# Projections of a hybrid decoder layer: one 512-column and one 256-column pass per weight block, rewritten as three 256-column passes into one set of columns

## The chip, the cores and the metric

The kernel runs on one core of one Trainium2 chip. The metric is the device time of one execution in microseconds, the median of several runs. Engines are named as the profile names them: PE is TensorE's matmuls, PEld its weight loads, DVE is VectorE, ACT ScalarE, POOL GpSimd, SP SyncE (it issues nearly all DMAs). In a matmul one operand is held in the array (the weights, loaded by a LDWEIGHTS) and the other moves through it, column by column.

## What is computed

One decoder layer on 256 tokens of width 2048, in float32. Cut to what matters here:

```python
h = rmsnorm(x, pre_mix_g)
proj = h @ w_in                       # q_a, k_a, v_a, q_b, k_b, v_b, f_b
o_a = swa_sink_attention(q_a, k_a, v_a, sinks)       # 16 heads of 64, 2 kv heads, window 128
o_b = forgetting_attention(q_b, k_b, v_b, log_f)     # 16 heads of 64
mix = concat(rmsnorm(o_a), rmsnorm(o_b)) @ w_out
x = x + rmsnorm(mix, post_mix_g)
h = rmsnorm(x, pre_ffn_g)
u = causal_dwconv(h @ w_up, conv_w, conv_b)          # w_up: 2048 x 11264, width 3
gate, val = split(u, 2)
y = (gelu(gate) * val) @ w_down                      # w_down: 5632 x 2048
return x + rmsnorm(y, post_ffn_g)
```

## The kernel before

**Numbers.** Products are made from float32r parts. A value x is split into hi (x rounded to float32r, a ScalarE copy) and lo (x - hi, a VectorE subtraction). A product is the sum of three: hi by hi, hi by lo, lo by hi.

**Layout.** The normalised activations stand transposed in hT: 16 K tiles (KT) of 128 rows, each with 512 columns, namely the high parts of the 256 tokens (0:256) and their low parts (256:512). Weights come from DRAM in units of up to 1024 floats per partition (w_load, into one of five raw buffers), are cast by ScalarE into whi and subtracted by VectorE into wlo (w_split, L120 and L123), five buffers each.

**Projections.** proj_T makes 256 output columns (two blocks m of 128) from four units of four K tiles each. The weights are held, hT moves. For every K tile and block, high() lets all 512 columns of hT pass the high weights into a bank of 512 columns: the left half collects hi by hi, the right half hi by lo. low() lets the 256 high columns pass the low weights into the right half of the same bank. So a projection uses two PSUM banks, one a block, and 32 matmuls of 512 columns (L264) and 32 of 256 (L271). In the feed-forward stage the order is LONG: high of units 0 and 1, low of all four, high of 2 and 3. In the attention stage it is high 0, 1, low 0, 1, high 2, 3, low 2, 3. The first two projections (keys and values, first queries) run through unit_T (L227, L232) interleaved with the arrival of x. The first gate projection of the feed-forward has an order of its own (first_gate, L911 and L916).

**Where the weights lie.** The high half starts at the start of its tile. The low half of a held unit starts LOW[i] * 4 floats into its tile, which is 128 floats longer than needed:

```python
LOW = (14, 4, 4, 4)
...
        at = LOW[unit[0] % period[0]] * 4
```

The counter starts anew with each projection; its period is four in the feed-forward stage and two in the attention stage.

**Evacuation.** Both halves of a bank have to be added and multiplied by the tokens' 1/rms, which is a row (rowq, rowk, rowf) because tokens are columns here. evac_sum (L417 to L419) and conv (L856 to L858) do it in three steps for each block: ScalarE copies the right half out, VectorE adds the left half to it, GpSimd multiplies by the row. Then come the split into parts (attention) or the convolution, GELU and gating (feed-forward).

**Other matmuls.** The values' projection, w_out and w_down let the weights move and hold activations (mm3 at L286, products at L1032). Some blocks of w_down go through a seven-product scheme (seven), for which GpSimd and VectorE make sums and differences beforehand; stage() prepares part of these in DRAM.

**Order.** TensorE's order is the program's (a manual schedule). tick() and later() place the attention's steps between the passes of projections. The other engines' order comes from the scheduler, pinned at some places. PSUM has four banks tagged acc and four tagged att; feed-forward projections alternate between the two.

Of the kernel before, what the change touches and what calls it, by code (L numbers as in the profile page):

```python
# [28 lines left out]
STORED = (((0, 0, 1), (0, 0, 3), (0, 0, 5), (0, 2, 1), (0, 2, 3), (0, 2, 5), (1, 0, 1)), ((1, 0, 3), (1, 2, 0), (1, 2, 1), (1, 2, 2)))  # L29
LOW = (14, 4, 4, 4)  # L30
ROOM = 112
# [3 lines left out]
def hybrid_layer(ctx: ExitStack, tc: tile.TileContext, x, pre_mix_g, w_in, b_forget, sinks,  # L35
# [42 lines left out]

    unit, period = [0], [2]

    def w_parts(n, keep=None, held=True):

        if keep and keep[0] is None:
            return keep[1]
        where, pre, nb = (keep[0], "h", keep[1]) if keep else (wp, "w", WB)
        hi = where.tile([P, UNIT], F32R, tag=pre + "hi", bufs=nb, name="whi")
        if where is not wp:
            lo = where.tile([P, UNIT], F32R, tag=pre + "lo", bufs=nb, name="wlo")
# [130 lines left out]

    def unit_T(parts, u, banks, ticks=True, halves=False):  # L220

        hi, lo = parts

        def high(a):
            kt = u * 4 + a
            for m, b in enumerate(banks):
                pe.matmul(b, hi[:, a, m * P:(m + 1) * P], hT[:, kt, 0:512], start=(kt == 0),  # L227
                          stop=(kt == KT - 1))

        def low(a):  # L230
            for m, b in enumerate(banks):
                pe.matmul(b[:, 256:512], lo[:, a, m * P:(m + 1) * P],  # L232
                          hT[:, u * 4 + a, 0:256], start=False, stop=False)
# [12 lines left out]
        if ticks:  # L246
            tick()

    def proj_T(w, c0, banks, runs=((0, 1), (0, 1), (2, 3), (2, 3))):

        parts, last = {}, ((len(runs) - 1) % 2, KT - 1)
        unit[0], period[0] = 0, 4 if len(runs) == 3 else 2

        def get(u):
            if u not in parts:
                parts[u] = w_split(w_load(w_rows(w, u * 4, 4, c0, 256), 4, 256))
            return parts[u]

        def high(u):
            hi = get(u)[0]  # L260
            for a in range(4):
                kt = u * 4 + a
                for m, b in enumerate(banks):
                    pe.matmul(b, hi[:, a, m * P:(m + 1) * P], hT[:, kt, 0:512], start=(kt == 0),  # L264
                              stop=(last == (0, kt)))

        def low(u):
            lo = get(u)[1]
            for a in range(4):
                for m, b in enumerate(banks):  # L270
                    pe.matmul(b[:, 256:512], lo[:, a, m * P:(m + 1) * P],  # L271
                              hT[:, u * 4 + a, 0:256], start=False,
                              stop=(last == (1, u * 4 + a)))
# [18 lines left out]
    with tc.tile_pool(name="mixp", bufs=1) as mp:  # L292
# [37 lines left out]
        def scratch():  # L330
            rot[0] += 1
            i = 6 + rot[0] % 10
            return scr[:, i * 256:(i + 1) * 256]

# [10 lines left out]
        warm_up(2)  # L345
        bkv = [bank("att"), bank("att")]
        bq0 = [bank(), bank()]
        for u in range(4):
# [72 lines left out]
        def q_pair(b):  # L421
            q = scratch()
            evac_sum(b, q, rowq)
            qh = ap.tile([P, 256], F32R, tag="qh", bufs=6, name="qh")
            ql = ap.tile([P, 256], F32R, tag="ql", bufs=6, name="ql")
            split(qh, ql, q)
            return qh, ql

        def k_pair(b, i):
            k = scratch()  # L430
            evac_sum(b, k, rowk)
            split(khi[i], klo[i], k)

        tiles = (1, slice(0, 256)), (0, slice(256, 384))

        def attend(j, q, ki, values, table, h0, sink, at):
# [53 lines left out]
            def pv():  # L490
# [10 lines left out]
                if sink:  # L501
                    half = ap.tile([64, 512], F32, tag="half", bufs=1, name="half")
                    act.copy(half, o[64:128, :])
                    ob = scratch()
                    for e in range(2):
# [65 lines left out]
        def kv_a():  # L571
            k32 = scratch()
            evac_sum(bkv[0], k32, rowk)
            ksw = scratch()
# [5 lines left out]
            v32 = scratch()  # L580
            evac_sum(bkv[1], v32, rowk)

# [10 lines left out]
        for g in range(4):  # L593
            if g == 0:
                b2 = bq0
            else:
                b2 = [bank(), bank()]
                proj_T(w_in, g * 256, b2)
            for m in range(2):
                swa_pair(2 * g + m, q_pair(b2[m]), stages(6 + 8 * g, m))  # L600

# [59 lines left out]
        for g in range(4):  # L661
            bq = [bank(), bank()]
            proj_T(w_in, 1280 + g * 256, bq)
            qs = [q_pair(b) for b in bq]
            bk = [bank(), bank()]
            proj_T(w_in, 2304 + g * 256, bk)
            for m in range(2):
                ki = (2 * g + m + 2) % NK
                k_pair(bk[m], ki)
                fox_pair(2 * g + m, qs[m], ki, stages(5, m))  # L670

# [112 lines left out]

        unit[0], period[0] = 0, 4

        def gate_unit(u):
# [34 lines left out]
    with tc.tile_pool(name="ffn", bufs=1) as fp:  # L822
# [21 lines left out]

        NU = 4
        ubuf = [fp.tile([P, 258], F32, tag=f"u{i}", name=f"u{i}") for i in range(NU)]
        for u in ubuf:
            pool.memset(u[:, 0:2], 0.0)
        cnt = [0]
        x_dram = tc.dram_tile([2 * P, D], F32, name="x_dram")  # L850

        def conv(b, ch, y):
            u = ubuf[cnt[0] % NU]
            cnt[0] += 1
            c = fp.tile([P, 256], F32, tag="cs", bufs=3, name="cs")
            act.copy(c, b[:, 256:512])  # L856
            dve.tensor_tensor(u[:, 2:258], b[:, 0:256], c, op=ALU.add)  # L857
            pool.tensor_tensor(u[:, 2:258], u[:, 2:258], rowf, op=ALU.mult)  # L858
            act.activation(y, u[:, 2:258], AF.Identity, bias=cw[:, 3, ch:ch + 1],  # L859
# [78 lines left out]
        for half in range(2):  # L938
            G = [fp.tile([P, 512], F32R, tag="G", bufs=FHALF, name=f"G{j}")[:, 0:512]
                 for j in range(FHALF)]  # L940
            most = max(len(at) for at in SEVENS[half])
            both = min(len(at) for at in SEVENS[half])
            sums = []

            def sums_at(u):
                w, at = 384 if u < both else 512, 768 * min(u, both) + 1024 * max(u - both, 0)
                if not u:
# [8 lines left out]
            for g in range(FHALF // 2):  # L956
                c0 = (half * (FHALF // 2) + g) * 256
                alt = (g + half) % 2
                if half == 0 and g == 0:
                    bg = first_gate()  # L960
                    order.__exit__(None, None, None)
                    bv = [bank(), bank()]
                    proj_T(w_up, DFF + c0, bv, LONG)
                else:
                    bg = [bank("att"), bank("att")] if alt else [bank(), bank()]
# [3 lines left out]
                for m in range(2):  # L969
                    y = conv(bg[m], c0 // P + m, yy[:, m, :])  # L970
                    act.activation(y, y, AF.Gelu_apprx_tanh)
                    gates.append(y)
                if half or g:
                    bv = [bank("att"), bank("att")] if alt else [bank(), bank()]
                    proj_T(w_up, DFF + c0, bv, LONG)
                ys = []
                for m in range(2):
                    y = conv(bv[m], 44 + c0 // P + m, yy[:, 2 + m, :])
                    dve.tensor_tensor(y, y, gates[m], op=ALU.mult)
                    ys.append(y)  # L980
                if g < most:
# [5 lines left out]
                    s2, s3, s4, s1 = (s[:, i * P:i * P + P] for i in range(4))  # L987
                    if g < both:
                        s1 = a21
# [54 lines left out]
            def seven(n, u, last, banks, opened):  # L1044
# [11 lines left out]
                s2, s3, s4, s1 = [  # L1056
                    [x[:, i * P:i * P + P] for x in sums[1 + u]] if i < 3 or u >= both
                    else parts_of(u * 2, 1) for i in range(4)]
# [164 lines left out]
        for n in range(4):  # L1223
            finish(0, slice(n * 512, (n + 1) * 512), r, sp)
        last = fp.tile([P, 256], F32, tag="cs", bufs=3, name="last")
        for h in range(2):
# [40 lines left out]
```

## Time and profile before

| what | value |
|---|---|
| time, median of 3 runs | 1053.36 us (1053.36 to 1053.54) |
| span of the profiled execution | 1051.2 us |
| PE busy | 1041.5 us (99%), 5896 matmuls |
| PEld busy | 907.5 us (86%), 5896 loads |
| DVE busy | 855.6 us (81%) |
| ACT busy | 647.8 us (62%) |
| POOL busy | 261.2 us (25%) |
| mean granted TensorE clock | 0.999 |
| moved by DMA | 238.82 MB |

The profiled execution's span is 2.2 us below the median time, which also has what lies around the span. Busy times are unions of an engine's instructions. A matmul's own duration runs to its modelled end, so matmuls overlap in the rows; how fast they follow each other is read from the starts, and in the view of the chain, whose pieces run from start to start. A row "x32" in the timeline merges 32 instructions of one line that follow each other.

### The profile page before, as it was taken

What the parts mean: (1) busy time and instruction counts of PE and PEld (TensorE: products, weight loads), DVE (VectorE), ACT (ScalarE), POOL (GpSimd) and SP (SyncE); (2) the same over time, 40 slices, a digit from 0 to 9 for tenths busy, and PEclk for the clock granted to TensorE, in tenths of its full rate; (3) what the DMA queues carried; (4) which work ended last, traced back from release to release, by engine and by line L of the source; (5) the groups of instructions that cost most, each with busy time, mean ns of one, the idle gap of its engine ahead of it and who ended that gap; (6) DMA issues with size and microseconds to landing.
All of it is one profiled execution on the core that took longest, in us unless ns stands there. A gap on an engine that the chain in (4) does not pass through costs nothing.

```text
span 1051.2 us, 16601 instructions
## 1 busy us (share of the span) xinstructions
PE 1041.5 (99%) x5896; PEld 907.5 (86%) x5896; DVE 855.6 (81%) x1407; ACT 647.8 (62%) x1109; POOL 261.2 (25%) x295
## 2 busy tenths in 40 slices
PE   9999999999999999999999999999999999999996
PEld 7889988888889988888888888888888888888886
DVE  5989877877467898989987988868888878799783
ACT  7777767676557655656555655646566565566561
POOL 4253235441122423232211000003433121200023
PEclk9999999999999999999999999999999999999999
DMA  8645666555874788888975876777767777768783
GB/s 293 195 122 176 180 201 187 181 163 161 299 242 147 261 276 278 264 273 267 306 232 160 269 270 226 248 236 222 228 214 249 249 222 229 231 194 271 243 301 123
DMA packets 187326, 238.82 MB, mean 227 GB/s; under 512 B 8268, under 2 KB 154988, under 8 KB 186348
## 3 DMA queue, kind: packets, MB, share of 16 engines
q1 hardware_dynamic: 186924, 237.37, 70.4%
q8 instruction: 46, 0.75, 0.3%
q10 hardware_dynamic: 320, 0.40, 0.1%
q14 instruction: 36, 0.29, 0.1%
HBM read 221.86 MB, written 15.75 MB: 226 GB/s over the span
## 4 chain that ended last, share of the span: by engine, by line
PE 98%; DVE 1%; issue 0%; ACT 0%; DVEq 0%; POOLq 0%; ACTq 0%
PE bank_acc L264 21%; PE bank_acc L1032 15%; PE bank_att L264 15%; PE bank_acc L286 13%; PE bank_acc L271 11%; PE bank_att L271 8%; PE bank_att L1032 5%; PE bank_att L286 1%; PE bank_att L452 1%; PE bank_att L487 1%; PE bank_att L496 1%; PE bank_acc L911 1%; PE bank_att L227 1%; PE bank_acc L227 1%; PE bank_att L498 0%; DVE wlo L123 0%
## 5 line engine op out<-in xcount | busy, mean ns | idle before, releaser
L123 DVE TENSOR_TENSOR wlo<-raw,whi 128x1024 fp32r<-128x1024 f32 (+3 forms) x317 | 390.7, 1244 | 76.2 <-ACT whi L120 69.0
L120 ACT CAST whi<-raw 128x1024 fp32r<-128x1024 f32 (+3 forms) x316 | 321.0, 1032 | 126.7 <-issue 49.0
L264 PE MATMUL bank_acc<-hT,whi 128*128 128x512 f32 x1024 | 245.5, 392 | 0.0
L264 PEld LDWEIGHTS bank_acc<-hT,whi 128*128 128x128 f32 x1024 | 188.2, 188 | 37.1
L858 POOL TENSOR_TENSOR u<-u,rowf 128x256 f32<-128x256 f32 x88 | 91.9, 1066 | 424.0 <-DVE u L857 421.1
L264 PE MATMUL bank_att<-hT,whi 128*128 128x512 f32 x704 | 165.7, 390 | 0.0
L264 PEld LDWEIGHTS bank_att<-hT,whi 128*128 128x128 f32 x704 | 130.6, 188 | 26.2
L1032 PE MATMUL bank_acc<-whi,G 128*128 128x512 f32 x424 | 139.8, 389 | 0.0
L271 PEld LDWEIGHTS bank_acc<-hT,wlo 128*128 128x128 f32 x1024 | 123.5, 188 | 3.2
L271 PE MATMUL bank_acc<-hT,wlo 128*128 128x256 f32 x1024 | 125.8, 278 | 0.0
L859 ACT ACTIVATE yy<-u,cw 128x256 f32<-128x256 f32 x88 | 53.0, 603 | 81.5 <-POOL u L858 81.5
L1032 PEld LDWEIGHTS bank_acc<-whi,G 128*128 128x128 f32 x424 | 79.6, 188 | 16.4
L271 PEld LDWEIGHTS bank_att<-hT,wlo 128*128 128x128 f32 x704 | 83.6, 188 | 1.9
L271 PE MATMUL bank_att<-hT,wlo 128*128 128x256 f32 x704 | 83.9, 277 | 0.0
L1032 PE MATMUL bank_acc<-wlo,G 128*128 128x512 f32 x212 | 82.5, 389 | 0.0
L286 PE MATMUL bank_acc<-whi,oT 128*128 128x512 f32 (+1 forms) x272 | 81.8, 379 | 0.0
L861 DVE SCALAR_TENSOR_TENSOR yy<-u,cw,yy 128x256 f32<-128x256 f32 x88 | 55.3, 634 | 13.9 <-ACT yy L859 13.6
L290 DVE TENSOR_TENSOR wlo<-raw,whi 128x1024 fp32r<-128x1024 f32 (+1 forms) x54 | 55.8, 1047 | 11.7 <-ACT whi L289 11.0
L289 ACT CAST whi<-raw 128x1024 fp32r<-128x1024 f32 (+1 forms) x54 | 47.8, 892 | 26.0 <-PE bank_acc L1032 16.8
L286 PEld LDWEIGHTS bank_acc<-whi,oT 128*128 128x128 f32 x272 | 50.2, 188 | 9.3
L286 PE MATMUL bank_acc<-wlo,oT 128*128 128x512 f32 (+1 forms) x136 | 51.2, 377 | 0.0
L286 PE MATMUL bank_acc<-whi,hT 128*128 128x384 f32 (+1 forms) x192 | 46.9, 323 | 0.0
(265 smaller groups left out, 1416.3 us busy)
## 6 DMA issues: line engine op xcount, KB each, us to landing
raw<-in_w_up_dram SPq DMA_DIRECT2D x176, 512.0 KB, 4.7
raw<-in_w_down_dram SPq DMA_DIRECT2D x68, 512.0 KB, 5.0
raw<-in_w_in_dram SPq DMA_DIRECT2D x51, 512.0 KB, 5.0
raw<-in_w_out_dram SPq DMA_DIRECT2D x32, 512.0 KB, 4.7
staged<-in_w_down_dram SPq DMA_DIRECT2D x44, 256.0 KB, 5.6
t_dram<-staged SPq DMA_DIRECT2D x22, 512.0 KB, 6.1
raw<-t_dram SPq DMA_DIRECT2D x14, 512.0 KB, 5.4
raw<-in_w_in_dram SPq DMA_DIRECT2D x16, 384.0 KB, 3.3
```

Of the source, the lines that this page charges most:

```text
L120: i1 = act.copy(hi[:, cs], raw[:, cs])
L123: i2 = dve.tensor_tensor(lo[:, cs], raw[:, cs], hi[:, cs].bitcast(F32), op=ALU.subtract)
L227: pe.matmul(b, hi[:, a, m * P:(m + 1) * P], hT[:, kt, 0:512], start=(kt == 0), stop=(kt == KT - 1))
L264: pe.matmul(b, hi[:, a, m * P:(m + 1) * P], hT[:, kt, 0:512], start=(kt == 0), stop=(last == (0, kt)))
L271: pe.matmul(b[:, 256:512], lo[:, a, m * P:(m + 1) * P], hT[:, u * 4 + a, 0:256], start=False, stop=(last == (1, u * 4 + a)))
L286: pe.matmul(b, a, r[:, cols], start=(first and i == 0), stop=(last and i == 2))
L289: act.copy(hi, src)
L290: dve.tensor_tensor(lo, src, hi.bitcast(F32), op=ALU.subtract)
L858: pool.tensor_tensor(u[:, 2:258], u[:, 2:258], rowf, op=ALU.mult)
L859: act.activation(y, u[:, 2:258], AF.Identity, bias=cw[:, 3, ch:ch + 1], scale=cw[:, 2, ch:ch + 1])
L861: dve.scalar_tensor_tensor(y, u[:, 1:257], cw[:, 1, ch:ch + 1], y, op0=ALU.mult, op1=ALU.add)
L1032: pe.matmul(b, x, r, start=b not in opened and not i, stop=closes and i == 2)
```

## The change

- proj_T and unit_T write into one bank: block m has columns m * 256 to m * 256 + 256. hi_rows makes two 256-column matmuls with the same high weights (hT's high columns, then its low columns) into the same columns; lo_rows makes the low one, again into these columns. All three products are thus summed in PSUM.
- High and low halves of a unit of w_parts share one tile, wboth, as long as the two tiles before. For held units the high half starts 16 floats (64 bytes) in, the low half at float 1024 + 80. LOW and its counter are gone. This holds for first_gate's weights too.
- evac and rows_of are one VectorE multiply of the 512-column bank by the row, which is broadcast over the two blocks. q_pairs and k_pairs handle two blocks at once. first_gate still has two banks and the three steps (sums_of).
- Scratch slots, the convolution's input tiles and the cs tile are cut anew; a small tile gap fills up the difference.

```diff
     def w_parts(n, keep=None, held=True):
...
-        lo = where.tile([P, UNIT + 128], F32R, tag=pre + "lo", bufs=nb, name="wlo")
-        at = 0
-        if held:
-            at = LOW[unit[0] % period[0]] * 4
-            unit[0] += 1
-        return hi[:, :n], lo[:, at:at + n]
+        both = wp.tile([P, 2 * UNIT + 128], F32R, tag="wboth", bufs=WB, name="wboth")
+        hi, lo = (16, UNIT + 80) if held else (0, UNIT)
+        return both[:, hi:hi + n], both[:, lo:lo + n]
...
+    def both(x, n):
+
+        return x.unsqueeze(1).to_broadcast([P, 2, n])
+
+    def hi_rows(b, hi, kt, last):
+
+        for m in range(2):
+            for i in range(2):
+                pe.matmul(b[:, m * 256:(m + 1) * 256], hi[:, m * P:(m + 1) * P],
+                          hT[:, kt, i * 256:(i + 1) * 256], start=(kt == m == i == 0),
+                          stop=last and m == i == 1, skip_group_check=True)
+
+    def lo_rows(b, lo, kt, last):
+
+        for m in range(2):
+            pe.matmul(b[:, m * 256:(m + 1) * 256], lo[:, m * P:(m + 1) * P], hT[:, kt, 0:256],
+                      start=False, stop=last and m == 1, skip_group_check=True)
...
         def high(u):
             hi = get(u)[0]
             for a in range(4):
-                kt = u * 4 + a
-                for m, b in enumerate(banks):
-                    pe.matmul(b, hi[:, a, m * P:(m + 1) * P], hT[:, kt, 0:512], start=(kt == 0),
-                              stop=(last == (0, kt)))
+                hi_rows(b, hi[:, a, :], u * 4 + a, last == (0, u * 4 + a))
 
         def low(u):
             lo = get(u)[1]
             for a in range(4):
-                for m, b in enumerate(banks):
-                    pe.matmul(b[:, 256:512], lo[:, a, m * P:(m + 1) * P],
-                              hT[:, u * 4 + a, 0:256], start=False,
-                              stop=(last == (1, u * 4 + a)))
+                lo_rows(b, lo[:, a, :], u * 4 + a, last == (1, u * 4 + a))
...
-        def evac_sum(b, dst, row):
-
-            c = scratch()
-            act.copy(c, b[:, 256:512])
-            dve.tensor_tensor(dst, b[:, 0:256], c, op=ALU.add)
-            pool.tensor_tensor(dst, dst, row, op=ALU.mult)
...
+        def evac(b, row):
+
+            dst = scratch()
+            dve.tensor_tensor(halved(dst), halved(b), both(row, 256), op=ALU.mult)
+            return dst
...
+        def rows_of(b):
+            u = ubuf[cnt[0] % NU]
+            cnt[0] += 1
+            dve.tensor_tensor(u[:, :, 2:258], b.rearrange("p (m c) -> p m c", m=2),
+                              both(rowf, 256), op=ALU.mult)
+            return [u[:, m, :] for m in range(2)]
...
```

More of the change, by code (lines that the diff above doesn't have):

```diff
@@ L84, in w_parts @@
             return keep[1]
[L85 to L88, printed above, removed]
+        if keep:
+            hi, lo = [keep[0].tile([P, UNIT], F32R, tag="h" + x, bufs=keep[1], name="w" + x)
+                      for x in ("hi", "lo")]
             return hi[:, :n], lo[:, :n]
-        lo = where.tile([P, UNIT + 128], F32R, tag=pre + "lo", bufs=nb, name="wlo")
-        at = 0
-        if held:
-            at = LOW[unit[0] % period[0]] * 4
-            unit[0] += 1
-        return hi[:, :n], lo[:, at:at + n]
+        both = wp.tile([P, 2 * UNIT + 128], F32R, tag="wboth", bufs=WB, name="wboth")
+        hi, lo = (16, UNIT + 80) if held else (0, UNIT)
+        return both[:, hi:hi + n], both[:, lo:lo + n]
     def w_high(unit, keep=None, held=True):
@@ L247, in unit_T, with proj_T @@
             tick()
-    def proj_T(w, c0, banks, runs=((0, 1), (0, 1), (2, 3), (2, 3))):
+    def proj_T(w, c0, b, runs=((0, 1), (0, 1), (2, 3), (2, 3))):
         parts, last = {}, ((len(runs) - 1) % 2, KT - 1)
-        unit[0], period[0] = 0, 4 if len(runs) == 3 else 2
         def get(u):
@@ L345, in hybrid_layer @@
         warm_up(2)
-        bkv = [bank("att"), bank("att")]
-        bq0 = [bank(), bank()]
+        bkv = bank("att")
+        bq0 = bank()
         for u in range(4):
@@ L503, in pv @@
                     act.copy(half, o[64:128, :])
[L504 removed]
+                    ob = scratch()[:, 0:256]
                     for e in range(2):
@@ L596, in hybrid_layer @@
             else:
-                b2 = [bank(), bank()]
+                b2 = bank()
                 proj_T(w_in, g * 256, b2)
-            for m in range(2):
-                swa_pair(2 * g + m, q_pair(b2[m]), stages(6 + 8 * g, m))
+            for m, q in enumerate(q_pairs(b2)):
+                swa_pair(2 * g + m, q, stages(6 + 8 * g, m))
         z = ap.tile([P, 2, H], F32, tag="z", name="z")
@@ L968, in hybrid_layer @@
                 yy = fp.tile([P, 4, 256], F32, tag="yy", bufs=2, name="yy")
-                for m in range(2):
-                    y = conv(bg[m], c0 // P + m, yy[:, m, :])
+                for m, u in enumerate(rows_of(bg) if half or g else sums_of(bg)):
+                    y = conv(u, c0 // P + m, yy[:, m, :])
                     act.activation(y, y, AF.Gelu_apprx_tanh)
@@ L973, in hybrid_layer @@
                 if half or g:
-                    bv = [bank("att"), bank("att")] if alt else [bank(), bank()]
+                    bv = bank("att") if alt else bank()
                     proj_T(w_up, DFF + c0, bv, LONG)
                 ys = []
-                for m in range(2):
-                    y = conv(bv[m], 44 + c0 // P + m, yy[:, 2 + m, :])
+                for m, u in enumerate(rows_of(bv)):
+                    y = conv(u, 44 + c0 // P + m, yy[:, 2 + m, :])
                     dve.tensor_tensor(y, y, gates[m], op=ALU.mult)
@@ L1224, in hybrid_layer @@
             finish(0, slice(n * 512, (n + 1) * 512), r, sp)
-        last = fp.tile([P, 256], F32, tag="cs", bufs=3, name="last")
+        last = fp.tile([P, 256], F32, tag="cs", bufs=1, name="last")
         for h in range(2):
```

92 lines of the change are left out of this document (44 added, 48 removed).

## The prediction

> **What bounds the kernel now.** I read the page's busy table first, then its clock row, the chain that ended last, and the costliest groups.
>
> ```profile
> PE 1041.5 (99%) x5896; PEld 907.5 (86%) x5896; DVE 855.6 (81%) x1407; ACT 647.8 (62%) x1109; POOL 261.2 (25%) x295
> ...
> PEclk9999999999999999999999999999999999999999
> ...
> PE 98%; DVE 1%; issue 0%; ACT 0%; DVEq 0%; POOLq 0%; ACTq 0%
> ...
> L264 PE MATMUL bank_acc<-hT,whi 128*128 128x512 f32 x1024 | 245.5, 392 | 0.0
> ...
> L264 PE MATMUL bank_att<-hT,whi 128*128 128x512 f32 x704 | 165.7, 390 | 0.0
> ...
> L271 PE MATMUL bank_acc<-hT,wlo 128*128 128x256 f32 x1024 | 125.8, 278 | 0.0
> ```
>
> TensorE is busy 99% of the span at full clock, it holds 98% of the chain, and its idle time before the projections' matmuls is 0.0. It is the bound nearly everywhere, so only a change in the spacing of its matmuls, or a new wait in it, moves the time. There are as many weight loads as matmuls (5896 each): a repeated weight is loaded again, so "held" saves no load. The mean durations (392, 278 ns) overlap each other; what counts is the distance from start to start. So next I read TensorE's timeline through one projection of the feed-forward stage, and from a second, narrower window the steady part of a low run.
>
> ```profile
> 364.19 7.45 PE L264 MATMUL bank_att<-hT,whi 128*128 128x512 f32 x32
> 371.48 3.82 PE L271 MATMUL bank_att<-hT,wlo 128*128 128x256 f32 x32
> 375.13 3.82 PE L264 MATMUL bank_att<-hT,whi 128*128 128x512 f32 x16
> 378.78 3.80 PE L264 MATMUL bank_acc<-hT,whi 128*128 128x512 f32 x16
> 382.42 3.82 PE L271 MATMUL bank_acc<-hT,wlo 128*128 128x256 f32 x32
> 386.07 0.40 PE L264 MATMUL bank_acc<-hT,whi 128*128 128x512 f32 x1
> ```
>
> ```profile
> 372.41 2.88 PE L271 MATMUL bank_att<-hT,wlo 128*128 128x256 f32 x24
> 375.13 0.40 PE L264 MATMUL bank_att<-hT,whi 128*128 128x512 f32 x1
> ```
>
> Two projections take 386.07 - 364.19 = 21.88 us, one 10.94 us: 32 high matmuls of 512 columns and 32 low ones of 256, with no hole between. A low run takes 375.13 - 371.48 = 3.65 us, 114.1 ns a matmul; its last 24 take 2.72 us, 113.33 ns each. The first eight cost 3.65 - 2.72 = 0.93 us, 116 ns each: an entry from high to low is dear. The chain in order of time gives the other spacings:
>
> ```profile
> 60.04 3.65 PE bank_acc L264 x16
> ...
> 76.60 0.66 PE bank_att L487 x6
> 77.26 5.21 PE bank_acc L286 x30
> ...
> 331.56 3.84 PE bank_acc L911 x32
> ...
> 576.54 6.80 PE bank_acc L1032 x30
> ...
> 1034.60 8.64 PE bank_att L286 x72
> ```
>
> Thirty 512-column matmuls (L1032) take 226.67 ns each, exactly 2 x 113.33; the 384-column ones (L286 at 77 us) 173.7. The 256-column ones of L911 and of L286 at the end take 3.84/32 = 8.64/72 = 120.0 ns, not 113.33. By the code, the weights of L911 and L286 begin at byte 0 of their tile or a multiple of 512 from it; those of the low runs begin 64 bytes in (LOW = 4, four floats each), in every fourth unit 224 bytes in. Six transposes with 128-column loads (L487) take 110 ns each, the closest spacing of full weight loads quoted here.
>
> **The change, part by part.**
>
> *High and low passes.* 54 projections go through proj_T (1728 high matmuls / 32) and two through unit_T: 56. Each has 32 pairs of (K tile, 128-column block); a pair is now one 512 and one 256 pass, and becomes three of 256. That adds 56 x 32 = 1792 matmuls and as many loads; the columns stay 768 a pair. The break-even is the mean of today's pair: 10.94 us / 96 = 113.96 ns per 256-column pass.
>
> The trace has no 256-column pass with high weights 64 bytes in, none that reads the second half of hT alone, and none whose weights lie where the low half now lies (float 1024 + 80, that is 64 bytes beyond an odd multiple of 256). Bounds: 110 ns (L487) below, 120.0 ns (L911) above. I take 113.33, the row nearest by far: same shape, same engine, same 64 bytes, 24 in a row. Three passes are then 340.0 ns, the same as 226.67 + 113.33: steady state against steady state, the change is worth nothing. What it takes away is the change from 512 to 256 and back.
>
> Feed-forward: 10.94 - 96 x 0.11333 = 0.06 us a projection, 43 of them: 2.6 us. In the attention stage the runs alternate twice as often and are shorter:
>
> ```profile
> 192.93 2.00 PE L271 MATMUL bank_acc<-hT,wlo 128*128 128x256 f32 x16
> 194.77 2.01 PE L264 MATMUL bank_acc<-hT,whi 128*128 128x512 f32 x8
> ```
>
> A low run of 16 takes 1.84 us against 1.813, a high one of 16 (the chain's 3.65 us) against 3.627. Two of each make 0.10 us a projection, 11 of them 1.1 us. The two unit_T projections alternate four times each, estimated at 0.05 us a time: 0.4 us. The first gate keeps its shapes but its 64 L911 passes get weights 64 bytes in: 64 x 6.67 ns = 0.4 us. Sum on the path: 4.5 us.
>
> *Evacuation.* Groups by shape:
>
> ```profile
> L858 POOL TENSOR_TENSOR u<-u,rowf 128x256 f32<-128x256 f32 x88 | 91.9, 1066 | 424.0 <-DVE u L857 421.1 <-DVE rowf L841 3.0
> ...
> L857 DVE TENSOR_TENSOR u<-bank_acc,cs 128x256 f32<-128x256 f32 x44 | 16.5, 416 | 0.0
> ...
> L856 ACT COPY cs<-bank_acc 128x256 f32<-128x256 f32 x44 | 14.3, 372 | 7.1 <-PE bank_acc L264 7.1
> ...
> L1021 DVE TENSOR_TENSOR y_sb<-bank_acc,y_sb 128x512 f32<-128x512 f32 x15 | 9.7, 682 | 6.4 <-PE bank_acc L1032 6.4
> ```
>
> A projection loses two ScalarE copies (0.74 us), two VectorE adds (0.83) and two GpSimd multiplies (2.13), and gains one VectorE multiply out of PSUM over 512 columns; the nearest row is L1021, 682 ns. For 43 projections that frees about 32 us of ScalarE, 6 of VectorE and 92 of GpSimd, and shortens the way from the last matmul to the convolution. All of it lies beside TensorE, so I cost it at 0. Were that cover gone, a projection's 0.68 us would be the price. One bank per projection where there were two only loosens PSUM.
>
> *Buffers.* High and low halves now share one tile and come free together, so ScalarE's cast for the unit five later may have to wait for the low pass, with GELU, convolution and G casts queued behind it. ScalarE's timeline:
>
> ```profile
> 473.09 1.99 ACT L120 CAST whi<-raw 128x1024 fp32r<-128x1024 f32 x2
> ...
> 478.84 1.05 ACT L120 CAST whi<-raw 128x1024 fp32r<-128x1024 f32 x1
> ...
> 480.32 1.06 ACT L120 CAST whi<-raw 128x1024 fp32r<-128x1024 f32 x1
> ```
>
> The first passes into bank_acc at 378.78 open a projection; eight steps of 10.94 us on, one starts at 466.3 and its first low unit ends at 470.9, the next at 471.8. The cast that reuses the first unit's buffer starts at 473.09, the second's at 474.04: later than the joint release already, so nothing waits that does not wait now. The cast done at 481.4 is used at the projection start of 488.2: 6.8 us of margin. Cost 0; to reach the path, casts would have to slip by several microseconds. No DMA is added, moved or removed; SP's queue keeps its order. The scratch, u and cs tiles are re-cut at nearly the same size: 0.
>
> The profiled execution spans 1051.2 us, 2.2 below the median of 1053.36. 1051.2 - 4.5 = 1046.7, in the metric **1048.9 us**. A difference under 0.2% (2.1 us) is about what cannot be told from no change.
>
> **The rivals.**
>
> *All passes settle on the slow spacing (slower).* That 64 bytes alone does not secure 113.33 is shown by two low runs of the first gate, weights 64 bytes in, between L911 passes:
>
> ```profile
> 340.36 1.11 PE L916 MATMUL bank_acc<-hT,wlo 128*128 128x256 f32 x8
> 341.31 3.04 PE L911 MATMUL bank_acc<-hT,whi 128*128 128x256 f32 x24
> 344.18 1.11 PE L916 MATMUL bank_acc<-hT,wlo 128*128 128x256 f32 x8
> ```
>
> 0.95 us for 8 is 118.5 ns. If the new passes stay there, 56 x 96 = 5376 passes cost 4.5 ns each over break-even: +24 us, 1078; at L911's 120.0, 1086. It decides from 113.96 ns on. For it: also that 226.67, 173.7 and 120.0 all stand 13 to 15 ns above their columns' share (53 ns per 128 columns), a price per matmul that splitting the high pass would pay twice. Against it: every long low run (24 after entry) sits at 113.33, so runs fall into it and remain.
>
> *Only the low half's new place is bad (slower).* Low passes at 120: 1792 x 6.67 ns = 11.9 us, net +7.4: 1061. No row speaks to that place.
>
> *Attention alone is slow.* Transposes and score matmuls break its runs; 13 projections at 118.5 against today's (2 x 3.65 + 2 x 1.84)/96 = 114.4 ns: +5.1, net of 3.0 in the rest +2.1: 1055.5.
>
> *A small fixed cost per matmul (no change).* 4.5 us / 1792 = 2.5 ns per added pass eats the gain: 1053. 226.67 = 2 x 113.33 speaks against it, though the two rows differ in where the weights lie. The Trainium skill's page "TensorE: Matmul & The Clock Gate", section "Back-to-back issue gap", gives N/2.4 + 2.5 ns: by that the added passes cost an estimated 4.5 us, and this rival holds. The trace does not bear out its level: it has 113.33 and 120.0 where the page has 109.2 for 256 columns.
>
> *The floor is the load (faster).* At L487's 110 ns, 5376 x 3.96 = 21 us: 1032. No 256-column row quoted is below 113.33.
>
> **How the numbers follow.** Steady 113.33: 0.55, its own range 1047 to 1051. Load floor 0.07; small fixed cost 0.08; attention slow 0.08; low half slow 0.10; all slow 0.12. Leaving out the first and the last of these others (0.19) gives 1040 to 1068. Faster 0.55 + 0.07, less a little for gains under 2.1 us: 0.60; same 0.12; slower 0.28.
>
> **What would show it.** TensorE's timeline through a feed-forward projection: 96 passes in 10.88 us, two projections in 21.76, no dear entries. Matmuls and loads 7688 each; GpSimd's busy time down by over 100 us; no L858-like group but for the first gate; TensorE still 98% of the chain. The prediction is wrong if passes stand at 118 to 120 ns anywhere for long, or if ScalarE's casts wait for TensorE long enough for TensorE to idle.

## The result, and the profile after

The changed kernel takes 1061.5 us (median of 4 runs, 1061.14 to 1062.95) against 1053.4 before: ratio 1.0078, 95% interval 1.0064 to 1.0092. It is 8.1 us slower, where 4.5 us faster was forecast.

The page of the changed kernel, its busy table and its chain that ended last:

```profile
PE 1049.0 (99%) x7688; PEld 988.8 (93%) x7688; DVE 823.3 (78%) x1343; ACT 618.1 (58%) x989; POOL 137.9 (13%) x182
...
PE 97%; DVE 1%; DMA 1%; ACT 0%; POOL 0%; SPq 0%; issue 0%; DVEq 0%; POOLq 0%; ACTq 0%
```

The count of matmuls and loads is the forecast one, the other engines are relieved as forecast (GpSimd by 123 us), and TensorE is still the bound. So the loss must stand in the spacing of its matmuls (the time from one start to the next) or in new waits of TensorE. The chain in order of time, pieces of 64 high passes (start, length, line):

```profile
365.66 7.25 PE bank_att L221 x64
...
921.23 7.54 PE bank_att L221 x64
```

In the feed-forward's first half every such piece takes 7.25 us, 113.3 ns a pass; in its second half every one takes 7.54, 117.8 ns. No piece lies between the two. TensorE's timeline through one projection of each half (start, length to the modelled end, line; L221 are high passes, L228 low ones):

```profile
372.75 3.79 PE L228 MATMUL bank_att<-hT,wboth 128*128 128x256 f32 x32
376.38 3.79 PE L221 MATMUL bank_att<-hT,wboth 128*128 128x256 f32 x32
380.01 0.73 PE L221 MATMUL bank_acc<-hT,wboth 128*128 128x256 f32 x5
```

```profile
702.47 3.93 PE L228 MATMUL bank_att<-hT,wboth 128*128 128x256 f32 x32
706.24 3.93 PE L221 MATMUL bank_att<-hT,wboth 128*128 128x256 f32 x32
710.00 0.75 PE L221 MATMUL bank_acc<-hT,wboth 128*128 128x256 f32 x5
```

3.63 us for 32 against 3.77: the same code and the same kinds of tiles, and high and low passes alike. By TensorE's landmarks (first matmul of a stage, after less before) the time goes as follows.

| stretch on TensorE | before, us | after, us | difference |
|---|---|---|---|
| start to the values' projection | 73.31 | 73.11 | -0.20 |
| values' projection | 55.05 | 55.05 | 0 |
| fox projections (queries and keys of the forgetting attention) | 107.11 | 107.97 | +0.86 |
| w_out | 95.92 | 95.89 | -0.03 |
| first gate | 13.74 | 14.53 | +0.79 |
| the other 21 projections of the first half | 230.57 | 229.30 | -1.27 |
| w_down, first half | 111.52 | 111.54 | +0.02 |
| 22 projections of the second half | 240.68 | 248.75 | +8.07 |
| w_down, second half, and the end | 123.26 | 123.42 | +0.16 |

The sum is 8.40 us of span. The two stretches of the feed-forward as the windows view gives them (first gate to w_down, and second half), before and after:

```profile
331.39:575.70 244.31, 244.30 (x1466) 216.85 (x1465) 215.98 (x359) 150.55 (x257) 67.87 (x74) 1.00 0.79 254
687.22:927.90 240.68, 240.68 (x1410) 212.55 (x1408) 193.91 (x297) 140.38 (x220) 60.86 (x62) 1.00 0.71 225
```

```profile
332.02:575.85 243.83, 243.16 (x2139) 242.13 (x2137) 203.03 (x340) 142.04 (x220) 19.13 (x34) 1.00 0.79 254
687.39:936.14 248.75, 248.75 (x2114) 248.75 (x2112) 184.96 (x276) 130.70 (x177) 13.27 (x20) 1.00 0.69 219
```

In the second half after the change TensorE is busy for all of the 248.75 us at full clock (1.00, the third column from the end): it waits for nobody.

### The profile page after: what moved, and what is told of

Its sections match the earlier page's. It is cut to its first block, busy times and chain, and to the rows that moved or that the text cites. A ratio compares the mean times of both kernels' runs of the same rounds, so it can differ in the third digit from the quotient of the medians.

```text
span 1059.6 us, 19834 instructions
## 1 busy us (share of the span) xinstructions
PE 1049.0 (99%) x7688; PEld 988.8 (93%) x7688; DVE 823.3 (78%) x1343; ACT 618.1 (58%) x989; POOL 137.9 (13%) x182
## 4 chain that ended last, share of the span: by engine, by line
PE 97%; DVE 1%; DMA 1%; ACT 0%; POOL 0%; SPq 0%; issue 0%; DVEq 0%; POOLq 0%; ACTq 0%
PE bank_acc L221 23%; PE bank_att L221 16%; PE bank_acc L1040 15%; PE bank_acc L228 12%; PE bank_acc L284 12%; PE bank_att L228 8%; PE bank_att L1040 5%; PE bank_att L452 1%; PE bank_att L284 1%; PE bank_att L487 1%; PE bank_att L496 1%; DMA x_in<-in_x_dram 1%; PE bank_att L498 0%; PE bank_acc L919 0%; PE bank_acc L924 0%; DVE hT L743 0%
## 5 line engine op out<-in xcount | busy, mean ns | idle before, releaser
L116 DVE TENSOR_TENSOR wboth<-raw,wboth 128x1024 fp32r<-128x1024 f32 (+3 forms) x317 | 378.7, 1209 | 127.4 <-ACT wboth L113 125.4
L113 ACT CAST wboth<-raw 128x1024 fp32r<-128x1024 f32 (+3 forms) x316 | 319.5, 1031 | 185.3 <-issue 50.8
L221 PE MATMUL bank_acc<-hT,wboth 128*128 128x256 f32 x2112 | 257.8, 279 | 0.0
L221 PEld LDWEIGHTS bank_acc<-hT,wboth 128*128 128x128 f32 x2112 | 249.8, 189 | 0.3
L221 PE MATMUL bank_att<-hT,wboth 128*128 128x256 f32 x1472 | 177.5, 279 | 0.0
L221 PEld LDWEIGHTS bank_att<-hT,wboth 128*128 128x128 f32 x1472 | 173.6, 189 | 0.1
L1040 PE MATMUL bank_acc<-wboth,G 128*128 128x512 f32 x636 | 153.5, 389 | 0.0
L1040 PEld LDWEIGHTS bank_acc<-wboth,G 128*128 128x128 f32 x636 | 119.1, 188 | 24.5
L228 PE MATMUL bank_acc<-hT,wboth 128*128 128x256 f32 x1056 | 131.1, 279 | 0.0
L228 PEld LDWEIGHTS bank_acc<-hT,wboth 128*128 128x128 f32 x1056 | 125.8, 188 | 0.1
L228 PE MATMUL bank_att<-hT,wboth 128*128 128x256 f32 x736 | 89.7, 279 | 0.0
L228 PEld LDWEIGHTS bank_att<-hT,wboth 128*128 128x128 f32 x736 | 87.2, 188 | 0.2 <-DVE wboth L116 0.2
L284 PE MATMUL bank_acc<-wboth,oT 128*128 128x512 f32 x336 | 78.0, 391 | 0.0
L284 PEld LDWEIGHTS bank_acc<-wboth,oT 128*128 128x128 f32 x336 | 62.6, 188 | 12.8
L288 DVE TENSOR_TENSOR wboth<-raw,wboth 128x1024 fp32r<-128x1024 f32 (+1 forms) x54 | 55.1, 1024 | 13.9 <-ACT wboth L287 13.0
```

What stands on the lines that cost most here:

```text
L113: i1 = act.copy(hi[:, cs], raw[:, cs])
L116: i2 = dve.tensor_tensor(lo[:, cs], raw[:, cs], hi[:, cs].bitcast(F32), op=ALU.subtract)
L221: pe.matmul(b[:, m * 256:(m + 1) * 256], hi[:, m * P:(m + 1) * P], hT[:, kt, i * 256:(i + 1) * 256], start=(kt == m == i == 0), stop=last ...
L228: pe.matmul(b[:, m * 256:(m + 1) * 256], lo[:, m * P:(m + 1) * P], hT[:, kt, 0:256], start=False, stop=last and m == 1, skip_group_check=True)
L284: pe.matmul(b, a, r[:, cols], start=(first and i == 0), stop=(last and i == 2))
L288: dve.tensor_tensor(lo, src, hi.bitcast(F32), op=ALU.subtract)
```

## Experiments

Theory A: 256-column passes with weights 64 bytes beyond a multiple of 256, counted from the start of their tile, have two spacings, 113.3 and 117.8 ns; a run (passes that follow each other with nothing else between) takes one at its entry and keeps it. Rival B: something in the second half itself (what runs beside it, where its tiles lie) makes it slow. Rival C: the low half's place, 64 bytes beyond an odd multiple of 256, does.

**One unit moved at the entry of the second half (e_first224).**

```diff
         hi, lo = (16, UNIT + 80) if held else (0, UNIT)
+        if held and once:
+            once.pop()
+            hi, lo = 56, UNIT + 120
...
+                    if half and not g:
+                        once.append(1)
                     proj_T(w_up, c0, bg, LONG)
```

> The changed kernel, with one unit alone moved: the first weight unit of the feed-forward's second half has its halves 224 instead of 64 bytes beyond a multiple of 256, as the kernel before had the first low unit of each run. Theory A: that unit's passes run near 117 ns and leave the run in the fast spacing, as they did in every low run before; the half then takes 22 x 10.88 = 239.4 us plus under 0.2, and the time falls by about 9.2 us to 1052. Theory B: the half stays at 248.8 us and the time at 1061.

Measured: 1051.96 us, ratio to before 0.9988 (0.9979 to 0.9998). TensorE's timeline at the entry:

```profile
687.30 3.85 PE L226 MATMUL bank_att<-hT,wboth 128*128 128x256 f32 x32
690.99 3.81 PE L233 MATMUL bank_att<-hT,wboth 128*128 128x256 f32 x32
694.64 7.42 PE L226 MATMUL bank_att<-hT,wboth 128*128 128x256 f32 x64
701.89 3.79 PE L233 MATMUL bank_att<-hT,wboth 128*128 128x256 f32 x32
705.52 3.79 PE L226 MATMUL bank_att<-hT,wboth 128*128 128x256 f32 x32
```

The first 32 passes take 3.69 us, the next 32 (the moved unit's 8 low ones among them) 3.65, and from 694.64 on all stand at 113.3: 7.25 us for 64, 3.63 for 32. Until w_down the half takes 239.44 us instead of 248.75. One unit of 88 decides 9.3 us; B falls. None of its ten executions lies above 1053.3 us.

**The reverse in the first half (e_mid0).** The same edit with offset 0 (hi, lo = 0, UNIT + 64) for the first unit of the first half's third gate projection.

> The changed kernel, with one unit alone moved in the first half of the feed-forward, where all passes stand at 113.3 ns: the first weight unit of the third gate projection gets offset 0 in place of 64 bytes. In the kernel before, low passes at 64 bytes behind passes at offset 0 and 120.0 ns stood at 118.5. Theory A (two spacings, kept from the entry): that unit's 24 passes take 120 ns, and all passes behind it up to the end of the half 117.8: some 18 projections of 11.31 us, the half up by about 8 us, the time about 1069. Rival (64 bytes falls into 113.3 by itself as long as nothing else runs): the passes are back at 113.3 within one projection, and the time is 1061.5.

Measured: 1069.25 us in one run. The timeline from the moved unit on:

```profile
380.26 3.96 PE L226 MATMUL bank_acc<-hT,wboth 128*128 128x256 f32 x32
384.06 3.94 PE L233 MATMUL bank_acc<-hT,wboth 128*128 128x256 f32 x32
387.85 7.70 PE L226 MATMUL bank_acc<-hT,wboth 128*128 128x256 f32 x64
395.38 3.93 PE L233 MATMUL bank_acc<-hT,wboth 128*128 128x256 f32 x32
```

From 387.85 on 64 passes take 7.53 us, 117.7 ns, and the passes keep this up to the end of the half, whose stage takes 251.56 us against 243.83. In an unbroken row of 256-column passes the slow spacing does not return to the fast one by itself.

**The low half's place (e_lo16).** `(16, UNIT + 80)` becomes `(16, UNIT + 16)`.

> The changed kernel, with the low half of a held unit at float 1024 + 16, so that both halves begin 64 bytes beyond a multiple of 512 (now the low one is 64 beyond an odd multiple of 256). Theory C (the low half's new place makes the slow spacing): the second half falls to about 239.4 us, the time to about 1052, and the attention stage is fast too. Theory A: the place modulo 512 does not matter; the two spacings stay 113.3 and 117.8, and the half is as before in one of them throughout (248.8 us if it is entered in the same way).

Measured: 1061.85 us, ratio 1.0085 (1.0068 to 1.0102); second half 248.74 us, its passes at 117.8. C falls: between these two places there is no difference.

**A break before each projection (e_break).** Six transposes of the identity before each projection of the second half.

> The changed kernel, with six 128-column transposes of the identity into an unused bank put on TensorE before each of the 22 projections of the feed-forward's second half. Their results are read by nobody. Theory A (two spacings; a run takes one of them when it is entered and keeps it until TensorE does something else): the 22 projections are no longer all at 117.8 ns; each stands at 113.3 or 117.8 ns from its first passes to its end, and which one changes only from projection to projection. Six transposes cost about 0.66 us and the entry 0.1, so the half takes 248.75 + 22 x 0.75 us less 0.43 us for each projection that turns fast. Theory B (the second half is slow for what runs beside it or where its tiles lie): all 22 stay at 117.8 ns.

Measured: 1076.18 us in one run; this expectation of A failed. All 22 projections stay slow. The timeline around one break:

```profile
699.90 0.82 PE L989 MATMUL bank_att<-ident 128*128 128x128 f32 x6
700.47 4.02 PE L221 MATMUL bank_att<-hT,wboth 128*128 128x256 f32 x32
704.33 3.93 PE L228 MATMUL bank_att<-hT,wboth 128*128 128x256 f32 x32
```

After the break 32 passes take 3.86 us, then 3.76: slow again each time. The run cannot tell whether this break leads back into the slow spacing or leaves it untouched; a break chosen blindly is no cure. Other breaks do change the spacing. In the changed kernel's attention stage runs behind transposes or scores came out both ways, in one and the same projection:

```profile
179.53 2.05 PE L228 MATMUL bank_acc<-hT,wboth 128*128 128x256 f32 x16
181.41 2.05 PE L221 MATMUL bank_acc<-hT,wboth 128*128 128x256 f32 x16
...
186.17 1.98 PE L228 MATMUL bank_acc<-hT,wboth 128*128 128x256 f32 x16
187.98 1.98 PE L221 MATMUL bank_acc<-hT,wboth 128*128 128x256 f32 x16
```

179.53 to 181.41 is 117.5 ns a pass; behind the matmuls at 183 to 184 us, 186.17 to 187.98 is 113.1. Each of the 16 runs of this stage keeps one of the two to its end, and in the traces of seven kernels with this same stage (the changed one and six of the experiments) each comes out the same way every time: here the outcome repeats and is not chance.

**Other offsets (e_off0, e_off128, e_off224).** Both halves of all held units at 0, 128 or 224 bytes beyond a multiple of 256: `(16, UNIT + 80)` becomes `(0, UNIT + 64)`, `(32, UNIT + 96)`, `(56, UNIT + 120)`.

> The changed kernel, with both halves of every held unit at offset 0 modulo 256 bytes in place of 64. If the offset sets the spacing, all projections' passes in both halves stand at 120.0 ns (as L911 before): 11.52 us a projection, both halves alike, 240 + 14 and 253.4 us; the time is about 1061.5 + 22 x 0.64 + 22 x 0.21 + 13 x 0.3 = 1084. If the offset does not matter, each half stands at 113.3 or 117.8.

> The changed kernel, with both halves of every held unit 128 bytes beyond a multiple of 256 in place of 64. No row shows this place for 256 columns. Theory A says nothing on the level; one spacing in both halves would mean that this place has no second state, 113.3 in both would make it the better place (time about 1051), 117.8 to 120 in both the worse (1071 to 1084).

> The changed kernel, with both halves of every held unit 224 bytes beyond a multiple of 256 in place of 64. In the low runs before, passes at this place took 113 to 120 ns, 117 in the mean, and left the run in the fast spacing. If that goes on without an end, both halves stand near 117 ns (11.23 us a projection) with no second state: time about 1061.5 + 22 x 0.35 - 22 x 0.08 = 1067. If such passes settle at 113.3 after their first few, both halves do, and the time is about 1051.

Measured, one run each: 1084.51, 1080.31 and 1069.21 us. The second halves, 32 low passes and the start of what follows:

```profile
744.34 4.00 PE L228 MATMUL bank_acc<-hT,wboth 128*128 128x256 f32 x32
748.18 4.00 PE L221 MATMUL bank_acc<-hT,wboth 128*128 128x256 f32 x32
```

```profile
735.11 3.90 PE L228 MATMUL bank_acc<-hT,wboth 128*128 128x256 f32 x32
738.84 3.90 PE L221 MATMUL bank_acc<-hT,wboth 128*128 128x256 f32 x32
```

Offset 0 (first fence) gives 3.84 us for 32, 120.0 ns, in both halves; its time met the expectation. Offset 128 stands at 120.0 in the second half and 118.5 to 118.8 in the first, within the worse case of its expectation. Offset 224 (second fence) gives 116.6 in the second half and 117.8 in the first, where the expectation had 117 in both. None of the three reaches 113.3 for long: of the four places only 64 bytes has it.

**The placement alone (e_place).** The kernel before with the change's w_parts; passes and evacuation as before.

> The kernel before, with the placement of the change alone: high and low halves of a unit in one tile, held units' halves 64 bytes in, LOW gone; passes of 512 and 256 columns and the evacuation in three steps as before. If the price above the columns' share belongs to each weight load and falls with the offset (13.3 ns at offset 0, 6.7 at 64, from 120.0 and 113.33 ns for 256 columns), the 512-column passes fall from 226.7 to 220 ns and the time by 1792 x 6.7 ns = 12 us to 1041. If it belongs to the columns, the 512-column passes stay at 226.7, and the time is that of the kernel before, 1053, within 3 us for the low runs' entries.

Measured: 1064.51 us, ratio 1.0104 (1.0089 to 1.0119): 11 us slower, where 12 us faster or no change stood. The timeline of a projection:

```profile
444.57 3.89 PE L260 MATMUL bank_acc<-hT,wboth 128*128 128x512 f32 x16
448.30 3.90 PE L260 MATMUL bank_att<-hT,wboth 128*128 128x512 f32 x16
452.04 3.79 PE L267 MATMUL bank_att<-hT,wboth 128*128 128x256 f32 x32
455.67 1.56 PE L260 MATMUL bank_att<-hT,wboth 128*128 128x512 f32 x6
```

16 high passes of 512 columns take 3.73 us, 233 ns each, against 226.7 with weights at offset 0. The low run takes 3.63 us with no dear entry. So this placement harms 512-column passes: 11.10 us a projection instead of 10.94. (It changes the offset and the tile together; no run has 512-column passes at 64 bytes in a tile of their own.) Over 43 projections that is some 7 of the 11 us; the rest was not followed up. Neither of the two ideas on the price holds.

This kernel has no unit at 224 bytes, and yet nearly all its low runs in the feed-forward are fast. The first of the second half is not:

```profile
699.39 3.93 PE L267 MATMUL bank_att<-hT,wboth 128*128 128x256 f32 x32
703.15 7.63 PE L260 MATMUL bank_att<-hT,wboth 128*128 128x512 f32 x32
710.62 3.80 PE L267 MATMUL bank_att<-hT,wboth 128*128 128x256 f32 x32
714.26 3.89 PE L260 MATMUL bank_att<-hT,wboth 128*128 128x512 f32 x16
```

It takes 3.76 us; the next, behind 32 passes of 512 columns, 3.64. A unit at 224 bytes is thus one way into the fast spacing, not the only one.

**The hole in the first gate, and a better version (e_pin, e_presplit, e_presplit_g1).** In the changed kernel's timeline TensorE waits in the first gate (a hole), and VectorE does a subtraction for the first value unit (L116) ahead of the residual's last steps:

```profile
336.79 2.64 PE L733 MATMUL bank_att<-ident,x_sb 128*128 128x128 f32 x16 [0.64 <-DVE x_sb L726]
```

```profile
327.21 1.22 DVE L116 TENSOR_TENSOR wboth<-raw,wboth 128x1024 fp32r<-128x1024 f32 x1
328.35 1.90 DVE L743 SCALAR_TENSOR_TENSOR hT<-bank_att,gcol,hT 128x128 fp32r<-128x128 f32 x7
```

All three kernels are e_first224 plus an edit. e_pin keeps the first value projection's casts and subtractions in program order:

```diff
-                parts[u] = w_split(w_load(w_rows(w, u * 4, 4, c0, 256), 4, 256))
+                parts[u] = w_split(w_load(w_rows(w, u * 4, 4, c0, 256), 4, 256), pin)
```

> The changed kernel with the one moved unit that puts the second half into the fast spacing, and with the casts and subtractions of the first value projection kept in program order on ScalarE and VectorE, so that none of them runs ahead of the residual's last steps. In the changed kernel one such subtraction (1.2 us) stands there, and TensorE waits 0.9 us for the residual. If that subtraction made the hole, the stage from the first gate to the first down-projection falls by about 1 us, and the time from 1052.0 to 1051.0. If the hole has another cause, the time stays at 1052.0.

Measured: 1053.08 us, ratio 1.0025 (1.0002 to 1.0049). The hole is gone (first gate 13.39 us), but the casts now come too late and two others open in the low passes of the first value projection:

```profile
352.95 1.21 PE L233 MATMUL bank_acc<-hT,wboth 128*128 128x256 f32 x8 [0.72 <-DVE wboth L121]
354.52 1.19 PE L233 MATMUL bank_acc<-hT,wboth 128*128 128x256 f32 x8 [0.37 <-DVE wboth L121]
```

Its 12 executions stand at two levels: 7 at 1052.0 to 1053.2 us, 5 at 1060.9 to 1061.7. A step of 9 us is what one half at 117.8 costs. That the first half took it behind these holes in those 5 is an inference; the profiled execution is one of the 7. Two variants of e_pin with 224 bytes in the attention stage moved that stage by -0.56 (e_pin_a0: first unit) and -0.31 us (e_pin_a02: first and third), within their expectations, and the time not beyond its interval (0.9999, 0.9985 to 1.0012; 1.0007, 0.9988 to 1.0026). They have the upper level too, in 1 of 11 and in 2 of 11 executions (1060.9 to 1061.3):

> As the run with pinned casts, and the first unit of each of the 11 projections of the attention stage at 224 bytes too. Theory A: after each interruption by transposes or scores a run takes one of the two spacings anew; a unit at 224 bytes helps only where a run is entered with it. The attention stage (107.97 us with fox projections and all, 1.1 us in it at stake for half of its passes being slow) changes by -1.5 to +0.5 us.

> As the run with pinned casts, and the first and third unit of each projection of the attention stage at 224 bytes, as the kernel before had its low halves. Half of the passes then stand near 117 ns, and the others are entered from them in the fast spacing: stage change -1 to +0.5 us against the run with pinned casts alone.

e_presplit writes out the first value unit's split at a better place instead, and e_presplit_g1 adds one unit at 224 bytes in the first half's second gate projection:

```diff
             lows[2]()
+            early.append(w_split(w_load(w_rows(w_up, 0, 4, DFF, 256), 4, 256)))
             x_squares(1)
...
-                    proj_T(w_up, DFF + c0, bv, LONG)
+                    proj_T(w_up, DFF + c0, bv, LONG, early)
```

> The changed kernel with the one moved unit of the second half, and with the first value unit's cast and subtraction written out behind the residual's last steps, before the squares of the second token block; the other units stay free. If the early subtraction made the hole, TensorE's 0.9 us wait in the first gate stage goes and no new wait comes: time 1050.9. If a hole is only exchanged for another, it stays near 1052. Where a new short wait falls into the first value projection, some executions may take the slow spacing in the first half (about 9 us more).

> As the run before, with the first unit of the first half's second gate projection at 224 bytes too. Theory A: whatever spacing the first value projection takes, this unit's passes at about 117 ns leave the rest of the half at 113.3: no execution stands 9 us above the others; a fast half pays 24 passes x 3.5 ns = 0.1 us.

Measured: e_presplit 1051.64 us, ratio 0.9982 (0.9974 to 0.9991), the lowest median of all, 0.2% below before; the stretch from the first gate to w_down falls from 243.84 us (e_first224) to 242.69, as expected for the hole, while the median fell by 0.3 us only, less than the executions spread (1050.7 to 1052.2). e_presplit_g1: 1051.74 us, 0.9983 (0.9974 to 0.9992); its stretch is 0.5 us longer than e_presplit's. None of the 11 executions of either stands 9 us above the rest, with or without the extra unit. The 0.5 us is not the unit's price, as TensorE's timelines show, first e_presplit, then e_presplit_g1:

```profile
336.51 2.51 PE L738 MATMUL bank_att<-ident,x_sb 128*128 128x128 f32 x16
...
339.10 1.98 PE L931 MATMUL bank_acc<-hT,wboth 128*128 128x256 f32 x16
340.92 0.84 PE L926 MATMUL bank_acc<-hT,wboth 128*128 128x256 f32 x6
```

```profile
345.81 3.93 PE L226 MATMUL bank_acc<-hT,wboth 128*128 128x256 f32 x32
349.58 1.11 PE L233 MATMUL bank_acc<-hT,wboth 128*128 128x256 f32 x8
350.53 0.47 PE L840 MATMUL bank_att<-ident,cst 88*128 88x88 f32 x4
350.83 0.64 PE L213 MATMUL bank_att<-diag,ones 128*128 128x128 f32 x4
...
354.05 3.79 PE L226 MATMUL bank_acc<-hT,wboth 128*128 128x256 f32 x32
357.68 3.84 PE L226 MATMUL bank_att<-hT,wboth 128*128 128x256 f32 x32
361.36 3.81 PE L233 MATMUL bank_att<-hT,wboth 128*128 128x256 f32 x32
365.01 7.42 PE L226 MATMUL bank_att<-hT,wboth 128*128 128x256 f32 x64
```

In e_presplit the passes behind the 16 transposes of the first gate are fast (1.82 us for 16). In e_presplit_g1 the same code there leaves them slow: 32 take 3.77 us at 345.81. The eight small matmuls at 350.53 then bring the fast spacing (3.63 at 354.05). Those some 100 slow passes make up most of the 0.5 us. The moved unit starts at 357.68, where the passes are fast already, and costs 3.68 + 3.65 against 2 x 3.63 us, the 0.1 expected; so it had nothing to switch in this execution. Two executions of the same code, up to there, took different spacings: at this place the code alone does not decide.

## Why the prediction was wrong

- **The bound, the counts, the evacuation: right.** TensorE alone sets the time. The one VectorE multiply takes 684 ns in the groups (682 taken from the nearest row) and costs TensorE nothing, as do the joint buffers in the second half: nothing makes TensorE wait there.
- **Steady 113.33 ns for all passes: the step that failed.** It held for the first half's 21 projections and failed for the second half's 22 and for part of the attention stage. The second half was put at -1.3 us and came at +8.07; its passes take 248.75 us / 2112 = 117.8 ns, above the break-even of 113.96.
- **The reading behind it.** The prediction argued that every long low run sits at 113.33, "so runs fall into it and remain". The first part is a fact of the trace. But every one of those runs had begun with a unit at 224 bytes, which LOW put there and the change removes. e_first224 shows that one such unit at the entry is enough, and e_mid0 that unbroken runs of 256-column passes do not fall into 113.3 by themselves. The changed kernel's first half is fast from the first gate's transposes on (16 passes behind them take 1.81 us). That the forecast held there was luck: in e_presplit_g1 the passes behind the same transposes stayed slow. The two L916 runs without such a unit, 118.5 ns in the prediction's fence, were the rows that matched the changed kernel; they were given to a rival at 0.12.
- **That rival** ("all passes settle on the slow spacing") had the right mechanism and break-even, and a spacing 0.7 ns too wide; starts rounded to 0.01 us do not tell 118.5 from 117.8 over 8 passes. Two halves entered differently were not among the cases.
- **What the change takes away was sized right where the spacing held:** 1.27 us over 21 projections, forecast 0.06 each. The reason given, that an entry from high to low passes is dear, is in part another one: the eight dear low passes (116 ns, some 0.02 of the 0.06 us) were those at 224 bytes, which cost 116.6 in e_off224, and e_place's low runs, entered from 512 columns without such a unit, take 3.63 us. The unit_T projections and the queries before the values' projection gave 0.20, where 0.4 + 3 x 0.10 was forecast.
- **Attention:** the eight fox projections came at +0.86 instead of -0.8. The rival with attention alone slow had 118.5 ns for all its passes; 472 of these 768 stand in runs at 117.8, the others at 113.3.
- **First gate:** +0.79 instead of -0.4. Joint buffers were costed at 0 and VectorE's order was taken as it stood; the scheduler's new order put 1.2 us ahead of a step TensorE waits for (why it chose this order is not shown). e_presplit gave 1.15 us back. With the hole gone the first gate takes 13.39 us, 0.35 less than before: its own term was right.
- **No fixed cost per matmul.** In the first half 96 passes take 10.88 us, the same as the steady 512 and 256 passes of before. What splitting a 512-column pass costs changes with the place of the weights: at offset 0 two passes of 256 take 240.0 ns where one of 512 takes 226.7; at 64 bytes they take 226.7 or 235.6 where one takes 233. The Trainium skill's formula for an isolated matmul ("TensorE: Matmul & The Clock Gate", "Back-to-back issue gap") would have made the added passes dearer by 2.5 ns each, wherever the weights lie; no run here shows that.

## What to carry to other kernels

A spacing read from a steady run holds only for runs entered the same way: before carrying it over, look at what stands ahead of each run that shows it, and give the rows without that preparation their full weight. A small table of offsets in a tuned kernel may be there for one unit in the sequence and not for its mean; removing it is a change of its own and is worth a run by itself. When a stage is slow throughout and another, of the same code, is fast throughout, suspect a spacing taken at the entry, and move one unit there to test it.

## What the runs showed of the hardware

- 256-column float32r passes, each with its own weight load, have a spacing that depends on where the weights lie in their tile. By bytes beyond a multiple of 256: 120.0 ns at 0, 118.5 to 120.0 at 128, 116.6 to 117.8 at 224, and 113.3 or 117.8 at 64. At 64 each of the two keeps itself for hundreds of passes (2112 in the second half). Passes at another offset (24 at 224 bytes to the fast one, 24 at 0 to the slow one) or matmuls of another kind in between can change it. Why is open; no run shows what lies below the spacing.
- 512-column passes go the other way: 226.7 ns at offset 0, 233 at 64. The Trainium skill ("TensorE: Matmul & The Clock Gate", "Step-by-step: what each phase is for") says that loading the next weights doesn't steal read bandwidth from the running matmul. The runs show that the spacing changes with the weights' address, even in passes twice as long as a 256-column one; whether the load slows the matmul or is itself the slower part, no run here separates.
- With the evacuation's GpSimd multiplies gone, a VectorE instruction that stayed became faster. In the groups before and after, the same instructions:

```profile
L861 DVE SCALAR_TENSOR_TENSOR yy<-u,cw,yy 128x256 f32<-128x256 f32 x88 | 55.3, 634 | 13.9 <-ACT yy L859 13.6
```

```profile
L869 DVE SCALAR_TENSOR_TENSOR yy<-u,cw,yy 128x256 f32<-128x256 f32 x88 | 38.8, 479 | 1.5 <-ACT yy L867 1.4
```

VectorE's convolution step falls from 634 to 479 ns, with 112 of the 114 GpSimd multiplies gone; in e_place, which keeps them, it takes 631. That GpSimd's work, and not another part of the evacuation, slowed it was not tested alone. The row makes 16.5 of the 32 us of busy time that VectorE lost, where about 6 were forecast for the feed-forward. It is worth nothing here, since TensorE is the bound.
